# Moving the forms of w_down into the mixer stage, and splitting the loads of the last stage in place

## The chip, the cores and the metric

One core of one Trainium2 chip. The metric is the time of one launch in microseconds on the device; below, "the time" is the median of the runs, and one further execution, taken with the hardware profiler, is where every row comes from.

## The reference, cut to what matters

One decoder layer over T = 1056 tokens (1024 of a prompt and 8 sequences of 4 new ones), D = 1024, all in float32.

```python
proj = x @ w_in                              # 1024 x 4096, split into hq hf hi hg rq rk rv rg
o_h  = hgrn2(silu(hq), k(hf), hi, logf(hf))  # 4 heads, chunkwise recurrence
o_r  = retention(rotary(rq), rotary(rk), rv) # 4 heads, chunkwise recurrence
mix  = concat(rmsnorm(o_h) * silu(hg), rmsnorm(o_r) * silu(rg))
x    = layer_norm(alpha * x + mix @ w_out)
hidden = silu(x @ w_gate) * (x @ w_up)       # 1024 -> 2816
x    = layer_norm(alpha * x + hidden @ w_down)   # 2816 -> 1024
```

The outputs are y for all tokens and the recurrent states of both head groups.

## The kernel before, in words

**Arithmetic.** Everything is kept transposed: 128 features in the partitions, tokens along the free dimension. A float32 operand is split by `split` (lines 205 to 207) into `hi`, a rounded copy in fp32r made by ScalarE, and `lo`, the remainder, made by VectorE or GpSimd. A product is then three matmuls, hi·hi, hi·lo and lo·hi.

**Stages.** (1) The mixer: `proj_rqk`, `proj_v` and `proj_hqf` project, head by head; `mixer`, a generator, does a head's recurrence. `gate` multiplies in the gates. (2) The output projection `oproj`, and the first layer norm. (3) Gate and up: FF = 2816 is 22 blocks of 128, taken as 11 pairs p. Pair 0 goes by `gu`; pairs 1 to 10 by `unit`, which multiplies 2 x 2 blocks by Strassen-Winograd's method with seven products (A11·B11, S2·T2, S3·T3, S1·T1, A12·B21, A22·T4, S4·B22) for each of two token halves `pr`. A unit has 7 x 2 x 12 = 168 matmuls, a pair two units (gate, then up). `blocks` makes the seven forms of the weights of a unit: it loads two raw blocks and makes sums on GpSimd (lines 876, 877, 878, 883) and seven splits. `kinds` makes the seven forms of the hidden activations and stores them in the DRAM tile `hd`. (4) Down: for each of seven products (`DOWN`), `wkind` loads four blocks of forms of w_down from the DRAM tile `wb`, `hkind` loads 11 blocks of `hd`, both are split again, and 4 x 33 matmuls run for each half, 1848 in all. The second layer norm, `norm2`, ends it.

**Forms of w_down, before.** `prep`, with `rowsum` and `forms`, works on them during gate and up. w_down is centred (each row minus its mean, which takes the layer norm's mean away beforehand). `rowsum` loads a row block whole for its sum; `forms` loads it again in halves, centres it and stores the seven forms, 14 stores to a pair. `forward` puts a piece of this into the queue `side` ahead of each unit.

**Order.** `side` is a queue of generators; `tick` takes steps from it between the matmul groups of the main work, so the code of both is interleaved as it is written. A scheduler with a timeline model of its own then fixes the order of the instructions on each engine; at run time every engine, and the one DMA queue (SP, which issues all loads and stores), keeps that order and waits at an instruction whose inputs or buffers are not ready. `high_priority` moves instructions up.

**Buffers.** Raw weights pass through `wr`, three buffers of 512 KB used in rotation by weights, `rowsum`, `forms` and `wkind` alike. Split weights pass through the ring `bh`/`bl` of eight half blocks. In PSUM, `pj` (three banks in the mixer, four later) holds projections, `mx` the rest. `h`, 16 buffers, holds hidden blocks and, in the last stage, the loads of `hkind`.

```python
side.append(("w", forward()))            # ahead of each unit of gate and up
w = blocks(a["w_gate"], 2 * p)
```

Of the kernel before, what the change touches and what calls it, by code (L numbers as in the profile page):

```python
# [9 lines left out]
F32 = mybir.dt.float32  # L10
# [17 lines left out]
H = 4  # L28
# [110 lines left out]
def body(tc, ctx, a):  # L139
# [73 lines left out]
    def load_raw(src, shape=(P, KT, P), part=None):  # L213
        raw = wp.tile(list(shape), F32, tag="wr", name="wr", bufs=3)
        nc.sync.dma_start(raw[:, :part] if part else raw, src)
        return raw
# [38 lines left out]
    with ExitStack() as ctxA:  # L255
# [22 lines left out]
        pa.tile([P, 744], F32, name="gap")  # L278
# [38 lines left out]
        def proj(mt, chunks=[(c * CW, CW) for c in range(NC3)]):  # L317
            w = pre.pop(mt) if mt in pre else load_w(a["w_in"][mt])
            for c0, n in chunks:
                out = pj()[:, :n]  # L320
                group(out, wk(w), xk(c0, n), rate[0])
                yield slice(c0, c0 + n), out
# [54 lines left out]
        def proj_rqk(h):  # L377
            q, k = (q0, k0) if h == 0 else (slot("q", 2), slot("k", 2))
            gens = [(proj(4 * H + h), q, 1.0), (proj(5 * H + h), k, P ** -0.5)]
# [32 lines left out]
        def wmean(k):  # L412
            wrow = load_raw(a["w_or"][k].rearrange("p (k n) -> p k n", n=P)).rearrange("p k n -> p (k n)")
            mn = tmp.tile([P, 1], F32, tag="mn", name="mn", bufs=2)
            V.tensor_reduce(mn, wrow, axis=AX, op=add)
            V.tensor_scalar(mn, mn, -1.0 / D, None, op0=mul)
            S.activation(wrow, wrow, AF.Identity, bias=mn)
            nc.sync.dma_start(wc[k], wrow)
# [248 lines left out]
        mix(1, 0)  # L667
        proj_rqk(1)
        mix(1, 1)
        proj_rqk(2)  # L670
        proj_v(1, 1)
# [5 lines left out]
        for k in range(3, 6):  # L677
            wmean(k)
        proj_hqf(0)
        for k in range(6, 8):  # L680
            wmean(k)
        proj_v(0, 0)
        mix(0, 0)
        proj_hqf(1)
        mix(0, 1)
        gate(1, 0)
        proj_hqf(2)
        proj_v(0, 1)
        mix(0, 2)
        gate(1, 1)  # L690
        proj_hqf(3)
        mix(0, 3)
# [15 lines left out]
    with ExitStack() as ctxB:  # L708
# [282 lines left out]
        def rowsum(p, i):  # L991
            raw = load_raw(a["w_down"][2 * p + i].rearrange("p (k n) -> p k n", n=P))
            mn = tmp.tile([P, 1], F32, tag=f"mn{i}", name=f"mn{i}", bufs=2)
            V.tensor_reduce(mn, raw.rearrange("p k n -> p (k n)"), axis=AX, op=add)
            V.tensor_scalar(mn, mn, -1.0 / D, None, op0=mul)  # L995
            if i == 0:
                mns[p] = [mn]
            else:
                both_ = tmp.tile([P, 1], F32, tag="mnb", name="mnb", bufs=2)
                V.tensor_tensor(both_, mn, mns[p][0], op=add)  # L1000
                mns[p] += [mn, both_]

        mns = {}

        def forms(p, c):
            m1, m2, m12 = mns[p]
            raw = wp.tile([P, 2, 2, 2, P], F32, tag="wr", name="wr", bufs=3)
            for i in range(2):
                nc.sync.dma_start(raw[:, i], a["w_down"][2 * p + i].rearrange("p (j c m n) -> p j c m n", j=2, c=2, n=P)[:, :, c])
            a11, a21, a12, a22 = [raw[:, i, j] for i in range(2) for j in range(2)]  # L1010

            def put(n, src):
                nc.sync.dma_start(wb[KW.index(n), 2 * c:2 * c + 2, :, p, :].rearrange("m p n -> p m n"), src)

            def two():
                return ut()[:, :2 * P].rearrange("p (m n) -> p m n", n=P)

            yield
            s1, s2, s4 = two(), two(), two()
            V.scalar_tensor_tensor(s1, a21, m12, a22, op0=add, op1=add)  # L1020
            put("S1", s1)
            V.tensor_tensor(a21, a11, a21, op=sub)
            put("S3", a21)
            yield
            for x, mn, n in ((a22, m2, "A22"), (a12, m2, "A12"), (a11, m1, "A11")):
                S.activation(x, x, AF.Identity, bias=mn)  # L1026
                put(n, x)
            V.tensor_tensor(s2, a22, a21, op=sub)
            put("S2", s2)
            yield  # L1030
            V.tensor_tensor(s4, a12, s2, op=sub)
            put("S4", s4)

        def prep():
            for i in range(2):
                rowsum(0, i)
            for p in range(NPAIR):
                for c in range(2):
                    for _ in forms(p, c):
                        yield  # L1040
                    if p + 1 < NPAIR:
                        rowsum(p + 1, c)
                    yield
                    if 2 * p + c > 1:
                        yield True

        def wkind(n, mm):
            out = []  # L1050
            for r0, r1 in ((0, 8), (8, NPAIR)):
                raw = load_raw(wb[n, mm, :, r0:r1, :], (P, 8, P), r1 - r0)
                if cnt["w"] < 2:
                    for r in range(r0, r1, HK):
                        e = min(r + HK, r1)
                        hi, lo = [t.rearrange("p (k n) -> p k n", n=P)[:, :e - r] for t in ring()]
                        split(hi, lo, raw[:, r - r0:e - r0])
                        out += [(hi[:, k], lo[:, k]) for k in range(e - r)]
                else:
                    s = (cnt["w"] - 2) % 6  # L1060
                    hi, lo = [X[:, hl].rearrange("p k t -> p (k t)")[:, (s * NPAIR + r0) * P:(s * NPAIR + r1) * P].rearrange("p (k n) -> p k n", n=P) for hl in range(2)]
                    split(hi, lo, raw[:, :r1 - r0])
                    out += [(hi[:, k], lo[:, k]) for k in range(r1 - r0)]
# [53 lines left out]
        work = prep()  # L1117

        def forward():
            for x in work:  # L1120
                yield
                if x:
                    return

        for p in range(1, NPAIR):
# [4 lines left out]
            side.append(("w", forward()))  # L1130
# [3 lines left out]
            side.append(("w", forward()))  # L1134
# [8 lines left out]
        for x in work:  # L1143
            pass
# [104 lines left out]
```

## Time and profile before

| | us |
|---|---|
| median of 3 runs | 1417.36 (1416.13 to 1419.42) |
| the profiled execution, its own time | 1416.91 |
| its span, first to last instruction | 1414.8 |
| PE busy in the span | 1307.9 (92%) |
| DVE, ACT, POOL busy | 793.9, 527.7, 688.5 |

PE is TensorE, PEld its weight loads, DVE VectorE, ACT ScalarE, POOL GpSimd, SPq the DMA queue on SyncE. A row of the timeline is: start, length, engine, line, operation, output tile <- inputs, shapes, count, and in brackets the idle time of the engine before it with what ended it. A granted clock of 1.00 is 2.4 GHz, of 0.50 1.2 GHz; a number between is a mean of these over a stretch. Instructions that overlap the edge of a window are counted in both windows.

### The profile page before, as it was taken

To read this page: it belongs to the slowest core of one execution; us is meant where nothing else is said; L and a number is where in the kernel's file an instruction comes from. 1 tells how busy PE (TensorE), PEld (TensorE's weight loads), DVE (VectorE), ACT (ScalarE), POOL (GpSimd) and SP (SyncE) were. 2 spreads that over 40 slices of the span, in tenths; PEclk is the share of its full clock that TensorE was granted. 3 is DMA by queue.
4 is the path that set the end of the run, shared out by engine and by line. 5 is a ranking of instruction groups with operands and counts; after the bars stand their busy time and mean duration, and the time that the engine had idled before them with its cause. 6 is when DMAs were issued, how large, how long until landed. Compare 5 with 4: busy or idle time off the path is not lost. (4 is left out here: it accounts for less than half of the span.)

```text
span 1414.8 us, 29994 instructions
## 1 busy us (share of the span) xinstructions
PE 1307.9 (92%) x11622; PEld 1276.2 (90%) x11622; DVE 793.9 (56%) x1759; ACT 527.7 (37%) x1192; POOL 688.5 (49%) x666
## 2 busy tenths in 40 slices
PE   8999999999999999999489889989999947999997
PEld 7999999899999999999479889989989937999997
DVE  6254643756666653876637545755665557543534
ACT  6242433323232342755132322233233343444553
POOL 2762421220222263737366775866676615666550
PEclk9999999999999999999799999999999978999998
DMA  7354311111221262222745445455546486566621
GB/s 266 131 187 166 122 48 58 66 48 49 77 62 34 61 174 84 76 81 75 236 142 185 154 151 176 159 171 173 166 152 194 137 248 188 177 197 186 183 92 62
DMA packets 173789, 190.71 MB, mean 135 GB/s; under 512 B 14800, under 2 KB 154960, under 8 KB 173648
## 3 DMA queue, kind: packets, MB, share of 16 engines
q1 hardware_dynamic: 173648, 188.81, 42.5%
q8 instruction: 91, 1.49, 0.5%
q14 instruction: 50, 0.41, 0.1%
HBM read 130.20 MB, written 58.56 MB: 133 GB/s over the span
## 5 line engine op out<-in xcount | busy, mean ns | idle before, releaser
L207 POOL TENSOR_TENSOR bl<-wr,bh 128x512 fp32r<-128x512 f32 x212 | 279.9, 1333 | 366.2 <-ACT bh L206 347.8
L242 PE MATMUL pj<-X,bh 128*128 128x352 f32 (+1 forms) x1936 | 427.4, 310 | 4.8 <-DVE q L388 3.3
L242 PEld LDWEIGHTS pj<-X,bh 128*128 128x128 f32 x1936 | 321.0, 189 | 9.4 <-issue 3.6
L242 PE MATMUL pj<-X,bl 128*128 128x352 f32 (+1 forms) x968 | 297.8, 308 | 0.1
L206 ACT CAST bh<-wr 128x512 fp32r<-128x512 f32 x226 | 134.6, 617 | 236.9 <-PE pj L242 67.6
L1156 PE MATMUL pj<-XB,X 128*128 128x264 f32 x1716 | 210.6, 285 | 0.0
L1156 PEld LDWEIGHTS pj<-XB,X 128*128 128x128 f32 x1716 | 209.2, 189 | 0.0
L242 PEld LDWEIGHTS pj<-X,bl 128*128 128x128 f32 x968 | 183.0, 189 | 0.8 <-DVE bl L207 0.4
L207 POOL TENSOR_TENSOR XB<-h,XB 128x264 fp32r<-128x264 f32 x154 | 123.3, 842 | 108.2 <-ACT XB L206 108.2
L901 PE MATMUL pj<-X,bh 128*128 128x264 f32 x672 | 126.3, 288 | 21.2 <-ACT bh L206 21.2
L901 PEld LDWEIGHTS pj<-X,bh 128*128 128x128 f32 x672 | 105.0, 190 | 21.8 <-ACT bh L206 21.6
L901 PE MATMUL mx<-XB,bh 128*128 128x264 f32 x608 | 114.6, 288 | 2.5 <-DVE mn L995 1.9
L901 PE MATMUL mx<-X,bh 128*128 128x264 f32 x608 | 114.3, 288 | 0.2 <-DVE mn L995 0.2
L901 PE MATMUL pj<-XB,bh 128*128 128x264 f32 x352 | 76.2, 317 | 26.3 <-ACT bh L206 26.3
L901 PEld LDWEIGHTS mx<-XB,bh 128*128 128x128 f32 x608 | 95.5, 192 | 3.4 <-DVE mn L995 2.5
L1026 ACT ACTIVATE wr<-wr,mn 128x256 f32<-128x256 f32 x66 | 32.5, 508 | 174.8 <-DMA wr<-in_w_down 83.0
L242 PE MATMUL pj<-bh,X 128*128 128x256 f32 x512 | 96.5, 284 | 0.0
L901 PE MATMUL pj<-X,bl 128*128 128x264 f32 x336 | 95.3, 286 | 0.1
L901 PEld LDWEIGHTS mx<-X,bh 128*128 128x128 f32 x608 | 94.5, 190 | 0.6 <-DVE mn L995 0.5
L207 DVE TENSOR_TENSOR X<-wr,X 128x1024 fp32r<-128x1024 f32 (+1 forms) x52 | 65.6, 1270 | 46.2 <-ACT X L206 35.8
L901 PEld LDWEIGHTS pj<-XB,bh 128*128 128x128 f32 x352 | 63.0, 218 | 28.5 <-ACT bh L206 28.5
L901 PE MATMUL mx<-X,bl 128*128 128x264 f32 x304 | 85.9, 285 | 1.8 <-POOL bl L207 1.8
(227 smaller groups left out, 2385.3 us busy)
## 6 DMA issues: line engine op xcount, KB each, us to landing
hd<-h SPq DMA_DIRECT2D x154, 132.0 KB, 1.9
h<-hd SPq DMA_DIRECT2D x154, 132.0 KB, 2.9
wr<-wb SPq DMA_DIRECT2D x28, 512.0 KB, 4.2
wr<-in_w_in SPq DMA_DIRECT2D x23, 512.0 KB, 3.7
wr<-in_w_gate SPq DMA_DIRECT2D x22, 512.0 KB, 4.1
wr<-in_w_up SPq DMA_DIRECT2D x22, 512.0 KB, 3.8
wr<-in_w_down SPq DMA_DIRECT2D x22, 512.0 KB, 3.6
wr<-in_w_down SPq DMA_DIRECT2D x44, 256.0 KB, 4.3
```

The lines of the kernel that those rows point to most:

```text
L206: S.copy(hi, src)
L207: (eng or V).tensor_tensor(lo, src, hi.bitcast(F32), op=sub)
L242: PE.matmul(out, l, r, start=(i == 0), stop=(i == n - 1))
L901: PE.matmul(bank[pr], l[:, k], rs[k][r], start=(first and n == 0), stop=(n == 3 * HK - 1), skip_group_check=not first)
L1026: S.activation(x, x, AF.Identity, bias=mn)
L1156: PE.matmul(out, l, r, start=(i == 0), stop=(i == 3 * NPAIR - 1))
```

## The change

1. `wforms(p)`, new, makes the forms of w_down of pair p between the heads of the mixer stage, eleven calls written into the list that orders the heads. It loads the two row blocks once (512 KB each, into `wr`), centres each with `center_rows` (the body of `wmean`, which stays in use for w_out), stores three forms as they are, makes the four others on GpSimd (one into the new tile `f1`, three in place) and stores them: 7 stores of 256 KB.
2. `rowsum`, `forms`, `prep`, `forward` and their places in gate and up are taken out.
3. `again` replaces `split` for the loads of the last stage: the DMA writes into the `lo` tile itself, ScalarE makes `hi` from it, and the remainder is made in place. So `wkind` needs no `wr` buffer and makes one load of 704 KB where it made two (the first two calls three loads into the ring), and `hkind` needs no `h` buffer. A load now waits until the matmuls that read the old content of that tile are done.
4. In `hkind` the remainders of the first 11 blocks, and of every second one of the next 11, are made on DVE instead of GpSimd.
5. In the first head's rotary projections the last three of six products go to `mx` banks instead of `pj`.

```diff
+        f1 = pa.tile([P, HK, P], F32, name="f1")
+        pa.tile([P, 232], F32, name="gap")
...
+        def proj(mt, chunks=[(c * CW, CW) for c in range(NC3)], banks=(None,) * NC3):
             w = pre.pop(mt) if mt in pre else load_w(a["w_in"][mt])
+            for (c0, n), bank in zip(chunks, banks + (None,)):
+                out = (bank or pj)()[:, :n]
...
+            b1, b2 = ((pj, pj, mx), (pj, mx, mx)) if h == 0 else ((pj,) * NC3,) * 2
+            gens = [(proj(4 * H + h, banks=b1), q, 1.0), (proj(5 * H + h, banks=b2), k, P ** -0.5)]
...
+        def center_rows(w):
+            flat = w.rearrange("p k n -> p (k n)")
             mn = tmp.tile([P, 1], F32, tag="mn", name="mn", bufs=2)
+            V.tensor_reduce(mn, flat, axis=AX, op=add)
             V.tensor_scalar(mn, mn, -1.0 / D, None, op0=mul)
+            S.activation(flat, flat, AF.Identity, bias=mn)
+
+        def wforms(p):
+            w1, w2 = [load_raw(a["w_down"][2 * p + i].rearrange("p (k n) -> p k n", n=P)) for i in range(2)]
+            a11, a21, a12, a22 = w1[:, :HK], w1[:, HK:], w2[:, :HK], w2[:, HK:]
+            def put(n, src):
+                nc.sync.dma_start(wb[KW.index(n), :, :, p, :].rearrange("m p n -> p m n"), src)
+            for w in (w1, w2):
+                center_rows(w)
+            put("A11", a11)
+            put("A12", a12)
+            put("A22", a22)
+            G.tensor_tensor(f1, a21, a22, op=add)
+            put("S1", f1)
+            G.tensor_tensor(a21, a11, a21, op=sub)
+            put("S3", a21)
+            G.tensor_tensor(a11, f1, a11, op=sub)
+            put("S2", a11)
+            G.tensor_tensor(a12, a12, a11, op=sub)
+            put("S4", a12)
...
         mix(1, 0)
+        wforms(0)
         proj_rqk(1)
         mix(1, 1)
+        wforms(1)
         proj_rqk(2)
+        wforms(2)
...
         proj_hqf(3)
+        wforms(10)
         mix(0, 3)
...
-        def rowsum(p, i):
...
-        def forms(p, c):
...
-        def prep():
...
+        def again(hi, lo, src, eng):
+            raw = lo.bitcast(F32)
+            nc.sync.dma_start(raw, src)
+            S.copy(hi, raw)
+            eng.tensor_tensor(lo, raw, hi.bitcast(F32), op=sub)

         def wkind(n, mm):
...
-                raw = load_raw(wb[n, mm, :, r0:r1, :], (P, 8, P), r1 - r0)
...
+                    s = (cnt["w"] - 2) % 6
+                    hi, lo = [X[:, hl].rearrange("p k t -> p (k t)")[:, s * NPAIR * P:(s + 1) * NPAIR * P] for hl in range(2)]
+                again(hi, lo, wb[n, mm, :, r:e, :].rearrange("p r n -> p (r n)"), V)
...
         def hkind(n, pr):
-                raw = hid(F32)
-                nc.sync.dma_start(raw, hd[n, pr, r])
...
-                split(hi, lo, raw, G)
+                again(hi, lo, hd[n, pr, r], V if cnt["h"] < NPAIR or cnt["h"] < 2 * NPAIR and r % 2 else G)
...
-            side.append(("w", forward()))
             w = blocks(a["w_gate"], 2 * p)
...
-            side.append(("w", forward()))
             unit(blocks(a["w_up"], 2 * p), (0, 1), up_fin(h, p), RF)
...
-        for x in work:
-            pass
```

## Rows read from the trace of the kernel before

**Rows 1.** The stages, by windows of the span. Columns: window, its length; then busy time and instructions of PE, PEld, DVE, ACT and POOL; granted TensorE clock; mean busy share of the DMA engines; GB/s.

```profile
25.00:475.00 450.00, 447.36 (x4867) 426.82 (x4866) 246.06 (x681) 152.54 (x329) 134.59 (x138) 1.00 0.27 87
690.00:715.00 25.00, 4.20 (x19) 3.90 (x20) 13.91 (x21) 2.71 (x7) 15.59 (x18) 0.52 0.62 199
...
715.00:1136.00 421.00, 385.07 (x2985) 379.43 (x2984) 245.92 (x419) 129.47 (x291) 291.00 (x234) 0.96 0.52 163
1136.00:1190.00 54.00, 24.16 (x172) 23.53 (x171) 35.09 (x42) 23.74 (x50) 25.04 (x35) 0.74 0.78 233
```

**Rows 2.** The chain that ended last, one stretch in the last stage, where PE runs matmuls of 264 columns with nothing else in between: start, length, what, count.

```profile
1358.48 36.77 PE pj L1156 x303
```

**Rows 3.** PE's timeline, from the end of pair 1 to the end of the hand-over to the last stage: the matmuls with an idle time before them that tell the periods apart, and the last one of pair 1 and of pair 10.

```profile
687.45 0.28 PE L901 MATMUL mx<-X,bl 128*128 128x264 f32 x1
...
710.69 1.25 PE L901 MATMUL pj<-X,bh 128*128 128x264 f32 x4 [21.20 <-ACT bh L206]
...
786.01 0.81 PE L901 MATMUL pj<-XB,bh 128*128 128x264 f32 x2 [3.54 <-ACT bh L206]
...
837.89 1.25 PE L901 MATMUL pj<-XB,bh 128*128 128x264 f32 x4 [4.88 <-ACT bh L206]
...
1075.27 0.51 PE L901 MATMUL pj<-XB,bh 128*128 128x264 f32 x2 [1.65 <-ACT bh L206]
...
1120.67 0.50 PE L901 MATMUL pj<-XB,bh 128*128 128x264 f32 x2 [1.76 <-ACT bh L206]
...
1139.52 0.28 PE L901 MATMUL mx<-X,bl 128*128 128x264 f32 x1
1160.83 0.81 PE L1156 MATMUL pj<-XB,bh 128*128 128x264 f32 x2 [21.04 <-ACT XB L206]
...
1187.82 0.78 PE L1156 MATMUL pj<-XB,bh 128*128 128x264 f32 x2 [8.80 <-DVE Y L1165]
```

**Rows 4.** Waits of PE, by line and releaser: total us, times, longest. The first row is of 690 to 1136 us (gate and up), the second, after the dots, the largest of 25 to 475 us (the mixer; its three rows add up to 2.4 us).

```profile
PE pj L901 <- ACT bh L206: 47.5, 11, 21.2
...
PE mx L652 <- DVE tk L625: 0.9, 1, 0.9
```

**Rows 5.** Waits of the DMA queue SP itself in 610 to 1140 us: total us, times, longest.

```profile
SPq L1013 <- DMA wr<-in_w_down: 51.9, 18, 4.8
SPq L215 <- POOL bl L207: 42.2, 18, 8.8
SPq L1013 <- ACT wr L1026: 34.5, 22, 4.8
```

**Rows 6.** SP's timeline in the long idle time of PE after pair 1.

```profile
699.91 3.88 SPq L961 DMA_DIRECT2D hd<-h  x5
...
704.86 0.92 SPq L215 DMA_DIRECT2D wr<-in_w_gate  x2
```

**Rows 7.** One set of weight forms from its load to its first and its last use: two rows of the chain (pair 10, up), and POOL's last split of the set in its timeline.

```profile
1110.52 5.33 DMA wr<-in_w_down
...
1120.69 1.28 POOL bl L207
...
1129.31 1.29 POOL L207 TENSOR_TENSOR bl<-wr,bh 128x512 fp32r<-128x512 f32 x1 [0.73 <-ACT bh L206]
```

**Rows 8.** Groups of instructions of one shape: line, engine, operation, tiles, shapes, count | busy us, mean ns of one | idle time before them and what ended it.

```profile
L207 POOL TENSOR_TENSOR bl<-wr,bh 128x512 fp32r<-128x512 f32 x212 | 279.9, 1333 | 366.2 <-ACT bh L206 347.8
L207 POOL TENSOR_TENSOR XB<-h,XB 128x264 fp32r<-128x264 f32 x154 | 123.3, 842 | 108.2 <-ACT XB L206 108.2
...
L206 ACT CAST XB<-h 128x264 fp32r<-128x264 f32 x154 | 55.4, 411 | 33.4 <-PE pj L1156 19.9 <-issue 10.7 <-DMA h<-hd 2.4
...
L790 POOL TENSOR_TENSOR Y<-Y,s 128x264 f32<-128x264 f32 x32 | 27.2, 883 | 2.3 <-ACT s L1142 2.3
...
L994 DVE TENSOR_REDUCE mn<-wr 128x1 f32<-128x1024 f32 x22 | 26.8, 1218 | 48.2 <-DMA wr<-in_w_down 48.2
...
L417 ACT ACTIVATE wr<-wr,mn 128x1024 f32<-128x1024 f32 x8 | 9.2, 1152 | 13.3 <-DVE mn L416 10.8 <-issue 1.2 <-POOL sg L387 1.1
```

**Rows 9.** The largest wait of SP in the mixer, 25 to 475 us: the store of a head's state waits for the recurrence.

```profile
SPq L590 <- DVE S L588: 133.4, 8, 32.1
```

**Rows 10.** The first rotary head: PE's wait for a PSUM bank within the first 30 us, and, after the dots, the window behind it.

```profile
PE pj L242 <- DVE q L388: 3.3, 1, 3.3
...
25.00:28.20 3.20, 3.20 (x13) 3.20 (x12) 2.81 (x10) 1.50 (x4) 0.24 (x1) 0.50 1.04 380
```

**Rows 11.** The hand-over to the last stage: the landing of the last store of hidden blocks, in the chain; SP's issue of the loads behind it; POOL and DVE in their timelines.

```profile
1153.96 5.70 DMA hd<-h
...
1154.95 12.29 SPq L1071 DMA_DIRECT2D h<-hd  x22
...
1160.85 25.04 POOL L207 TENSOR_TENSOR XB<-h,XB 128x264 fp32r<-128x264 f32 x35 [30.25 <-ACT XB L206]
...
1171.80 14.51 DVE L207 TENSOR_TENSOR X<-wr,X 128x384 fp32r<-128x384 f32 x1 [10.59 <-ACT X L206]
```

**Rows 12.** DMA issues: what, queue, operation, count, KB each, median us from issue to landing.

```profile
hd<-h SPq DMA_DIRECT2D x154, 132.0 KB, 1.9
h<-hd SPq DMA_DIRECT2D x154, 132.0 KB, 2.9
...
wc<-wr SPq DMA_DIRECT2D x8, 512.0 KB, 3.3
```

More of the change, by code (lines that the diff above doesn't have):

```diff
@@ L211, in ring, with load_raw @@
         return [wp.tile([P, HK * P], F32R, tag=t, name=t, bufs=RING) for t in ("bh", "bl")]
-    def load_raw(src, shape=(P, KT, P), part=None):
+    def load_raw(src, shape=(P, KT, P)):
         raw = wp.tile(list(shape), F32, tag="wr", name="wr", bufs=3)
-        nc.sync.dma_start(raw[:, :part] if part else raw, src)
+        nc.sync.dma_start(raw, src)
         return raw
@@ L276, in body @@
         csts.append(pa.tile([P, a["csm"].shape[1]], F32, name="csm"))
-        pa.tile([P, 744], F32, name="gap")
+        f1 = pa.tile([P, HK, P], F32, name="f1")
+        pa.tile([P, 232], F32, name="gap")
         xr = [slot(f"M{k}", 1) for k in range(KT)]
@@ L412, in wmean @@
         def wmean(k):
-            wrow = load_raw(a["w_or"][k].rearrange("p (k n) -> p k n", n=P)).rearrange("p k n -> p (k n)")
+            w = load_raw(a["w_or"][k].rearrange("p (k n) -> p k n", n=P))
+            center_rows(w)
+            nc.sync.dma_start(wc[k], w.rearrange("p k n -> p (k n)"))
+        def center_rows(w):
+            flat = w.rearrange("p k n -> p (k n)")
             mn = tmp.tile([P, 1], F32, tag="mn", name="mn", bufs=2)
-            V.tensor_reduce(mn, wrow, axis=AX, op=add)
+            V.tensor_reduce(mn, flat, axis=AX, op=add)
             V.tensor_scalar(mn, mn, -1.0 / D, None, op0=mul)
-            S.activation(wrow, wrow, AF.Identity, bias=mn)
-            nc.sync.dma_start(wc[k], wrow)
+            S.activation(flat, flat, AF.Identity, bias=mn)
[5 more added lines that the diff above has]
+            for w in (w1, w2):
+                center_rows(w)
+            put("A11", a11)
[9 more added lines that the diff above has]
+            put("S4", a12)
         def msplit(gi, sl):
@@ L678, in body @@
             wmean(k)
+        wforms(3)
         proj_hqf(0)
@@ L681, in body @@
             wmean(k)
+        wforms(4)
         proj_v(0, 0)
         mix(0, 0)
+        wforms(5)
         proj_hqf(1)
         mix(0, 1)
+        wforms(6)
         gate(1, 0)
+        wforms(7)
         proj_hqf(2)
+        wforms(8)
         proj_v(0, 1)
         mix(0, 2)
+        wforms(9)
         gate(1, 1)
         proj_hqf(3)
+        wforms(10)
         mix(0, 3)
@@ L987, in gu @@
                 V.tensor_tensor(f, po[1], sg, op=mul)
-        def rowsum(p, i):
[L992 to L1001, printed above, removed]
@@ L1003, in body @@
-        mns = {}
-        def forms(p, c):
[L1006 to L1032, printed above, removed]
@@ L1034, in prep @@
-        def prep():
[L1035 to L1045, printed above, removed]
+        def again(hi, lo, src, eng):
+            raw = lo.bitcast(F32)
+            nc.sync.dma_start(raw, src)
+            S.copy(hi, raw)
+            eng.tensor_tensor(lo, raw, hi.bitcast(F32), op=sub)
@@ L1049, in wkind @@
         def wkind(n, mm):
             out = []
-            for r0, r1 in ((0, 8), (8, NPAIR)):
-                raw = load_raw(wb[n, mm, :, r0:r1, :], (P, 8, P), r1 - r0)
+            for r in range(0, NPAIR, HK if cnt["w"] < 2 else NPAIR):
                 if cnt["w"] < 2:
[L1054 to L1058, printed above, removed]
+                    e = min(r + HK, NPAIR)
+                    hi, lo = [t[:, :(e - r) * P] for t in ring()]
@@ L1059, in wkind @@
                 else:
+                    e = NPAIR
                     s = (cnt["w"] - 2) % 6
-                    hi, lo = [X[:, hl].rearrange("p k t -> p (k t)")[:, (s * NPAIR + r0) * P:(s * NPAIR + r1) * P].rearrange("p (k n) -> p k n", n=P) for hl in range(2)]
-                    split(hi, lo, raw[:, :r1 - r0])
-                    out += [(hi[:, k], lo[:, k]) for k in range(r1 - r0)]
+                    hi, lo = [X[:, hl].rearrange("p k t -> p (k t)")[:, s * NPAIR * P:(s + 1) * NPAIR * P] for hl in range(2)]
@@ L1064, in wkind @@
+                again(hi, lo, wb[n, mm, :, r:e, :].rearrange("p r n -> p (r n)"), V)
+                out += [(hi[:, k * P:(k + 1) * P], lo[:, k * P:(k + 1) * P]) for k in range(e - r)]
             cnt["w"] += 1
@@ L1116, in body @@
                 side.insert(min(len(side), 1 if q == 1 else NQ), (("c1", q // 2), combine1(q // 2)))
-        work = prep()
-        def forward():
-            for x in work:
-                yield
-                if x:
-                    return
         for p in range(1, NPAIR):
@@ L1142, in body @@
                 S.copy(mc, mu)
-        for x in work:
-            pass
         last = []
```

4 lines of the change are left out of this document (removed).

## The prediction

> **What bounds the kernel now.** I read the windows by stage first, then PE's waits, then PE's timeline at the two places where it stands still longest, and last what the queues did there. PE sets the time. One 264-column matmul, back to back, takes 36.77 / 303 = 0.1213 us [rows 2], and that pace is the measure for what follows. In the mixer PE is busy 447 of 450 us, its waits add up to 2.4 us, and DVE, ACT and POOL are busy 55%, 34% and 30% [rows 1, 4]: room there, on every engine but PE. In gate and up it is different. From the last matmul of pair 1 (687.7) to the last of pair 10 (1139.8) are 452.1 us [rows 3]; nine pairs of 336 matmuls are 3024 x 0.1213 = 366.8, the small mean products about 2. **83 us are lost**, of which 21.2 in one hole, at 689.5 to 710.7. PE's waits in this stretch name one cause, ACT's cast of a weight form: 47.5 us in 11 waits, the hole among them [rows 4]. The granted clock is 0.52 in the window of the hole and 0.96 in the rest of the stage [rows 1]: the clock fell to 1.2 GHz behind the longer waits, and that is the remainder of the loss.
>
> Why are the casts late? In the hole SP issues stores of hidden blocks and of forms one behind the other, and the load of the next gate block goes out only at 704.9 [rows 6]. Over the whole stage SP itself waits 51.9 and 34.5 us at line 1013, the stores of the w_down forms, and 42.2 us at line 215, a raw load that waits for a `wr` buffer [rows 5]. Forms and unit weights share one in-order queue and three buffers. POOL is busy 291 of 421 us in this stage [rows 1], close behind PE.
>
> At the hand-over to the last stage PE stands 21.0 us, runs a little, and stands 8.8 us more [rows 3]. From 1139.8 to the end of the last matmul at 1401.1 are 261.3 us; 1848 x 0.1213 = 224.2, side products about 3.4, so **34 us are lost** here. The chain shows the order: last store of hidden blocks issued at about 1153.5, landed at 1159.7, the loads behind it; meanwhile the 22 loads are issued one by one over 12.3 us, POOL then makes 35 remainders in a row over 25.0 us, and a DVE remainder of the weights takes 14.5 us beside it [rows 11].
>
> **The change, part by part.**
>
> *First head, `mx` banks.* PE waits 3.3 us for a `pj` bank that the rotary products hold, and the 3.2 us window behind it runs at a granted clock of 0.50, which is another 1.6 us [rows 10]. With three `mx` banks the fourth product need not wait; it reads tokens that the third already read. The fifth needs the last third of x, whose split ends about when the fourth product has just begun. I take -4.9 us; bounds 0 (x or the first `pj` of `proj_v` is late instead) and -4.9.
>
> *Forms in the mixer.* Eleven calls add 22 loads, 22 reductions of 1.22 us on DVE, 22 centrings of 1.15 us on ACT, 44 sums on POOL (128x512, as the split remainder of that size, 1.33 us) and 77 stores [rows 8]: DVE 27 us, ACT 25 us, POOL 59 us. DVE goes from 246 to 273 of 450 us, POOL from 135 to 194; DMA traffic rises by 11 x (1.0 + 1.8) MB, some 70 GB/s beside 87 [rows 1]. The cover is PE's work in the mixer and the ring, which holds four weights ahead. The nearest precedent is `wmean`: eight loads, reductions, centrings and stores run in this stage already, and PE's waits there are 2.4 us in all [rows 4]. What is new is that POOL waits: the third sum overwrites a block whose store must have been read out, 3.3 us by the store of w_out's rows [rows 12], and behind POOL's sum stand the remainders of the next weights and, in heads 1 to 3, a rotary product that holds a `pj` bank. Three such heads, some 2 us each not hidden, make +6. Bounds: 0, as with `wmean`; and 11 x (2 x 1.22 of DVE + one longest wait behind a store) at half exposure, 11 x 5.7 / 2 = +31.
>
> *Gate and up without forms.* Taken from SP in this stage are 66 loads and 154 stores, from DVE and ACT their work on them, from `wr` all but the unit weights. The hole goes: what stood ahead of the gate load was a piece of `prep` three times the usual size. What then sets the pace? From 1110.5, with the loads of a set out, POOL's remainder of S2 is done at 1122.0 and that of the last form at 1130.6: 20.1 us [rows 7], with the buffer then free for the second load of the next unit, about 0.4 us for its issue. A unit of 168 matmuls is 20.4 us. So this chain stands level with PE, and it gets shorter by the part of the load that was slowed by the forms' traffic (5.3 us against about 4). Between 1075.3 and 1120.7, a pair without `center`, the period is 45.4 us where PE needs 40.8; between 786.0 and 837.9, one with it, 51.9 [rows 3]. `center` is 8 x 0.88 = 7.1 us of POOL [rows 8]. After the change I expect a plain pair at 1 us over PE's time and one with `center` at 4 over, since about 3 of its 7 us fit where POOL waits for loads: five plain pairs and four with it, 5 + 16, and 3 us at the start. So 24 of the 83 us stay: **-59 us**. Bounds: -83, PE never waits; and -28, only the hole with its clock goes: seven pairs from 786.0 to 1120.7 take 334.7 us where 286 are needed, 7 lost in each, 55 in the eight from pair 3 on, and 83 less these are 28.
>
> *Hand-over.* The loads no longer follow 35 splits on POOL: of the first 22 remainders DVE makes 16 and POOL 6. The tiles of T2 and T3 that the first 11 loads fill come free after the second and third product of the last unit, so ten of the eleven can be in place before it ends. What stays is the last block: its store lands in 1.9, its load in 2.9 us [rows 12], cast and remainder 0.4 and up to 0.8 [rows 8], against 30 matmuls or 3.6 us on the ten before it. With the issues between them that is about 4 us of wait if SP is free; with SP behind the last pair's stores and the lower clock after it I take 11 us lost of 34: **-22 us**. Bounds: -30 (4 stay) and -3, if the loads still stand behind the last store on SP. The queue must take 4 + 11 loads in any case, and all but the ring's now wait for PE where they used to wait for a buffer.
>
> The DVE remainder of 14.5 us [rows 11] bears on this. The Trainium skill (SBUF — State Buffer, section "Who interferes with whom") says that DVE and GpSimd share a port pair by an exclusive lock: a DVE instruction with two SBUF inputs and a GpSimd one that reads SBUF do not overlap, the later one stands still. The trace agrees: that remainder ended when POOL's row of 35 did. By the rule the 16 and the 6 follow one another, at POOL's 0.72 us each 22 x 0.72 = 16 us, against 16 x 0.72 = 12 if they overlapped; and the page speaks against the mixer part too, where 59 us of POOL sums would hold up DVE's recurrence.
>
> *The rest of the last stage.* In-place loads wait for PE to be done with a tile. 24 tiles hold two products' blocks, so a set has one product time, 4 x 33 x 0.1213 = 16 us, for load (2.9) and 11 remainders on POOL (11 x 0.84 = 9.3) [rows 8, 12]: 12.2 us fit. I put 0; if they did not fit, each of 12 later sets would show a wait.
>
> **The sum.** -4.9 + 6 - 59 - 22 = -80 us. The profiled execution took 1416.9 us by its own time (span 1414.8), half a microsecond below the median, so the sum goes from 1417: **1337 us**.
>
> **The rivals.**
>
> *The chain of the unit weights keeps the pace.* Speaks for it: POOL has the largest load after PE in this stage, and 20.1 us against 20.4 leaves nothing [rows 1, 7]. Against: SP's waits at line 1013, 86 us, go in any case [rows 5]. Only the hole goes then, -28 instead of -59: **1368 us**. Chance 0.20.
>
> *The hand-over stays.* For it: the order on SP is fixed beforehand, and the stores of `kinds` have high priority. -3 instead of -22: **1356 us**. Chance 0.12.
>
> *Everything lost in gate and up is the forms'.* -79 there and -28 at the hand-over, the mixer as with `wmean`: 1417 - 4.9 - 79 - 28 = **1305 us**. Chance 0.13.
>
> *Slower: the forms block the mixer.* One mechanism, SP in order. SP waits there 133 us for heads' states, up to 32.1 us at once [rows 9]. If such a store stands between a call's loads and its stores, POOL waits at the third sum as long, and with it the remainders of the next weights, beyond what the ring holds. At an average wait of 16.7 us (133.4 / 8) [rows 9] in each of 11 calls it costs 184 us, less the 86 gained elsewhere: **1515 us**. It decides from 86 / 11 = 7.8 us a call. Against: the ring's four weights cover more than that, and `wmean` stood in the same queue at no cost. Chance 0.05.
>
> My forecast has 0.50. **Range** 1303 to 1373: it takes in the forecast's own bounds in part, the fast case and both slower savings, and leaves out the blocked mixer and the ends of the mixer's cost. A measurement of this kernel can tell about 0.2%, 3 us, from no change. Faster has the first three cases and the forecast, 0.94; slower 0.05; same 0.01.
>
> **What would show it.** In the profile after: no PE wait over 5 us between pair 1 and pair 10, plain pairs within 42 us; PE's waits in the mixer under 10 us in all; no 14 us remainder and less than 12 us of PE's idle time at the hand-over; no wait at the fourth product. It would be wrong if POOL's sums stood waiting for stores while PE waited for a weight in the mixer, or if the pairs kept 45 us with POOL never idle.

## The result, and the profile after

The kernel after takes **1324.9 us** in the median of 4 runs (1321.4 to 1328.1) against 1418.1 us before; the ratio is 0.934, its 95% interval 0.932 to 0.937. The forecast was 1337 us with a range of 1303 to 1373. The profiled execution of after has a span of 1322.7 us, 92.1 less than before. The stages of the two profiles, cut where PE (TensorE) starts the first product of pair 1 and where it ends the last products of pair 10 and of the last stage:

| stage | before, us | after, us | difference | forecast |
|---|---|---|---|---|
| first head | | | -4.9 (measured alone, first experiment) | -4.9 |
| up to pair 1, from 641.8 with the banks alone | 646.6 | 666.6 | +24.8 | +6 |
| pairs 1 to 10 | 493.2 | 410.6 | -82.5 | -59 |
| from there to the last product | 261.3 | 231.8 | -29.5 | -22 |

The windows of the same stages in the kernel after, in the columns of [rows 1]:

```profile
25.00:475.00 450.00, 426.87 (x4680) 405.35 (x4679) 273.99 (x693) 166.46 (x335) 189.05 (x181) 0.98 0.50 156
667.00:1077.00 410.00, 410.00 (x3366) 409.73 (x3365) 209.44 (x374) 134.01 (x283) 323.65 (x268) 1.00 0.32 104
1077.00:1102.00 25.00, 20.73 (x169) 20.30 (x168) 24.74 (x45) 13.82 (x26) 13.45 (x14) 1.00 0.89 295
1102.00:1309.00 207.00, 207.00 (x1716) 207.00 (x1715) 89.64 (x184) 90.61 (x192) 107.45 (x132) 1.00 0.50 159
```

In gate and up PE is busy in all of 410 us, at a granted clock of 1.00, where it was 0.96 and 0.52 in the hole [rows 1]. The mixer pays: PE is idle for 23 of its 450 us, where it was for 2.6 [rows 1]. PE's largest waits there, 25 to 520 us (total, times, longest):

```profile
PE mx L610 <- ACT tk L593: 7.3, 4, 3.8
PE mx L497 <- DVE ain L526: 5.5, 3, 2.7
PE mx L497 <- DVE k L522: 2.6, 2, 2.2
PE pj L242 <- ACT v L354: 2.2, 2, 1.7
PE mx L681 <- DVE tk L654: 1.9, 1, 1.9
```

All of PE's waits there add up to 22.7 us, against 2.4 before. None of these is a weight that comes late. All but one row are small products of the recurrence that wait for DVE or for ACT (whose `tk` copies a transposed `k`); the row of line 242 is a projection that waits for ACT's copy out of its `pj` bank. The waits are some 20 of the 24.8 us. The rest goes with the clock: it is 0.50 in four short stretches of this stage, 13.7 us together, each within 1.5 us of the end of such a wait; from 291.0 to 294.2, two products of 352 columns take 0.79 us instead of 0.48. At the hand-over [rows 3], PE's timeline of after shows no idle time between the last product of pair 10 and the first of the last stage, and two short waits behind:

```profile
1076.91 0.28 PE L941 MATMUL mx<-X,bl 128*128 128x264 f32 x1
1077.03 0.40 PE L1127 MATMUL pj<-XB,bh 128*128 128x264 f32 x2
...
1087.33 0.39 PE L1127 MATMUL pj<-XB,bl 128*128 128x264 f32 x1 [2.62 <-DVE bl L1035]
...
1097.76 0.52 PE L1127 MATMUL pj<-XB,bh 128*128 128x264 f32 x2 [1.65 <-DVE Y L1136]
```

### The profile page after: what moved, and what is told of

It reads as the page before. It is cut to its first block, busy times and chain, and to the rows that moved or that the text cites. A ratio compares the mean times of both kernels' runs of the same rounds, so it can differ in the third digit from the quotient of the medians.

```text
span 1322.7 us, 29630 instructions
## 1 busy us (share of the span) xinstructions
PE 1281.9 (97%) x11622; PEld 1255.1 (95%) x11622; DVE 735.1 (56%) x1650; ACT 525.0 (40%) x1122; POOL 733.2 (55%) x694
## 4 chain that ended last, share of the span: by engine, by line
PE 80%; DMA 9%; DVE 5%; ACT 2%; issue 2%; POOL 2%; SPq 1%; ACTq 0%; POOLq 0%; DVEq 0%
PE pj L242 25%; PE mx L941 17%; PE pj L1127 16%; PE pj L941 14%; DMA wr<-in_w_in 2%; DMA wc<-wr 2%; DMA wb<-wr 1%; PE mx L640 1%; DMA wr<-in_w_down 1%; PE mx L610 1%; PE mx L497 1%; PE mx L242 1%; PE mx L642 1%; DVE mn L423 1%; DMA wr<-in_w_v 1%
## 5 line engine op out<-in xcount | busy, mean ns | idle before, releaser
L242 PE MATMUL pj<-X,bh 128*128 128x352 f32 (+1 forms) x1888 | 417.3, 309 | 4.6 <-ACT v L354 2.2
L242 PEld LDWEIGHTS pj<-X,bh 128*128 128x128 f32 x1888 | 313.9, 189 | 9.4 <-ACT v L354 2.6
L242 PE MATMUL pj<-X,bl 128*128 128x352 f32 (+1 forms) x944 | 290.9, 308 | 0.1
L206 ACT CAST bh<-wr 128x512 fp32r<-128x512 f32 x220 | 131.6, 619 | 284.1 <-POOL wr L918 70.9
L242 PEld LDWEIGHTS pj<-X,bl 128*128 128x128 f32 x944 | 178.4, 189 | 1.0 <-DVE bl L207 0.4
L1035 POOL TENSOR_TENSOR XB<-XB 128x264 fp32r<-128x264 f32 x138 | 114.8, 867 | 105.0 <-ACT XB L1034 104.4
L941 PEld LDWEIGHTS pj<-X,bh 128*128 128x128 f32 x672 | 104.3, 188 | 0.3
L941 PE MATMUL mx<-XB,bl 128*128 128x264 f32 x304 | 86.2, 283 | 0.0
L242 PEld LDWEIGHTS pj<-bh,X 128*128 128x128 f32 x512 | 80.0, 190 | 1.8 <-issue 1.5
L1034 ACT CAST XB<-XB 128x264 fp32r<-128x264 f32 x154 | 57.3, 411 | 39.8 <-PE pj L1127 20.5
L423 DVE TENSOR_REDUCE mn<-wr 128x1 f32<-128x1024 f32 x30 | 36.5, 1216 | 64.1 <-DMA wr<-in_w_down 47.2
```

What stands on the lines that cost most here:

```text
L206: S.copy(hi, src)
L242: PE.matmul(out, l, r, start=(i == 0), stop=(i == n - 1))
L423: V.tensor_reduce(mn, flat, axis=AX, op=add)
L941: PE.matmul(bank[pr], l[:, k], rs[k][r], start=(first and n == 0), stop=(n == 3 * HK - 1), skip_group_check=not first)
L1034: S.copy(hi, raw)
L1035: eng.tensor_tensor(lo, raw, hi.bitcast(F32), op=sub)
```

## The experiments

All runs in one table: where pair 1 starts, how long pairs 1 to 10 take, how long it is from there to the end of the last product (all from the trace), the median time, and the ratio to the kernel before with its interval. The first three columns are of one execution each; where the mixer is the same code (before, e3, e9, e11), pair 1 starts at 645.9 to 647.9, so differences of some 2 us there say nothing.

| run | pair 1 starts | pairs 1-10 | rest | median | ratio |
|---|---|---|---|---|---|
| before | 646.6 | 493.2 | 261.3 | 1418.1 | |
| after | 666.6 | 410.6 | 231.8 | 1324.9 | 0.934 [0.932, 0.937] |
| e1_banks | 641.8 | 494.6 | 258.9 | 1410.2 | 0.996 [0.994, 0.999] |
| e2_forms | 673.5 | 410.6 | 245.9 | 1343.5 | 0.949 [0.944, 0.955] |
| e3_inplace | 645.9 | 493.3 | 230.8 | 1387.1 | 0.981 [0.976, 0.986] |
| e4_pool | 667.1 | 410.6 | 229.0 | 1322.3 | 0.934 [0.930, 0.939] |
| e5_nosum | 657.2 | 410.6 | 233.0 | 1321.8 | 0.931 [0.929, 0.934] |
| e6_nocenter | 670.1 | 410.6 | 231.6 | 1326.2 | 0.935 [0.933, 0.937] |
| e9_free_store | 647.9 | 474.8 | 253.8 | 1389.2 | 0.979 [0.976, 0.982] |
| e11_nosumload | 647.7 | 449.6 | 249.8 | 1363.5 | 0.963 [0.960, 0.966] |
| e8_late | 675.2 | 410.6 | 233.2 | 1336.0 | 0.943 [0.941, 0.945] |
| e8_vlate | 673.8 | 410.6 | 232.8 | 1331.3 | 0.939 [0.936, 0.941] |
| e12_oneload | 662.6 | 410.6 | 232.7 | 1319.0 | 0.931 [0.927, 0.936] |
| e13_transfers | 642.0 | 410.6 | 233.1 | 1302.6 | 0.920 [0.917, 0.923] |

**The parts one by one.** Part 5 alone:

```
 before
-                out = pj()[:, :n]
+                out = (bank or pj)()[:, :n]
...
+            b1, b2 = ((pj, pj, mx), (pj, mx, mx)) if h == 0 else ((pj,) * NC3,) * 2
```

> The kernel before with part 5 alone (three of the first head's six rotary products in mixer banks). Theory: the wait of 3.3 us at the fourth product and the one of about 1.6 us behind it go, the first product of proj_v starts at 31.6 us instead of 36.6 and everything behind it keeps its distance: -5 us, about 1412. Rival: the mixer banks so taken make the first transposes wait, and the gain is given back before 60 us: 1416 to 1419.

Pair 1 starts 4.9 us earlier. The median falls by 7.6 against the runs of before beside it; the interval, 2 to 9 us, holds the 5. The theory stands.

The forms alone, the last stage and the banks as before (of the edit, the hidden blocks' loads are shown):

```
 after
-                again(hi, lo, hd[n, pr, r], V if cnt["h"] < NPAIR or cnt["h"] < 2 * NPAIR and r % 2 else G)
+                raw = hid(F32)
+                nc.sync.dma_start(raw, hd[n, pr, r])
+                split(hi, lo, raw, G)
...
```

> The kernel before with the forms of w_down made between the mixer heads, but its own loads of the last stage (through wr and h, the splits of the activations on GpSimd) and its own banks. Theory: the mixer costs +25 us, pairs 1 to 10 give -82.5, and of the 29.5 us of the hand-over only the third that hung on SP's queue and on the forms' last stores comes (-9), since the 35 GpSimd operations ahead of the second group stay: about 1351. Rival: the whole of the hand-over was SP's queue behind the forms' stores: about 1330.

Parts 3 and 4 alone, the in-place loads with the splits on DVE (forms still in gate and up):

```
 before
+        def again(hi, lo, src, eng):
...
-                raw = hid(F32)
-                nc.sync.dma_start(raw, hd[n, pr, r])
-                split(hi, lo, raw, G)
+                again(hi, lo, hd[n, pr, r], V if cnt["h"] < NPAIR or cnt["h"] < 2 * NPAIR and r % 2 else G)
```

> The kernel before with parts 3 and 4 alone: loads of the last stage split in place, the first activations' splits on DVE; the forms are made in the gate/up stage as before. Theory: gate/up and mixer unchanged, the first product of the last stage not earlier (the forms' last stores still stand in SP's queue), the GpSimd wait of 21 us in the second group shortens to under 3: about -18, 1399. Rival: the loads still come behind the forms' stores, so DVE's splits start as late as GpSimd's did: 1412 to 1417.

And the kernel after with part 4 undone:

```
 after
-                again(hi, lo, hd[n, pr, r], V if cnt["h"] < NPAIR or cnt["h"] < 2 * NPAIR and r % 2 else G)
+                again(hi, lo, hd[n, pr, r], G)
```

> The kernel after with all splits of the activations left on GpSimd (part 4 undone, loads still in place). Theory: 11 splits at about 0.84 us are 9.3 us for a stage whose first group multiplies for 16 us, and SP's queue is free now, so GpSimd falls behind in the first group only: +5 to +10, 1330 to 1335. Rival 1: GpSimd was the whole of the hand-over, +20, 1345. Rival 2: with the queue free GpSimd keeps up: 1325.

The forms alone give the whole 82.5 us of pairs 1 to 10 and, with the banks as before, cost 26.8 in the mixer. At the hand-over both theories missed, since two different changes reach the same loss: the forms' move gives 15.3 us of it, the in-place loads give 30.5 by themselves, with the forms' stores still in the queue. Splitting on GpSimd alone (e4) is no worse than splitting on DVE: rival 2 there. The first loads of hidden blocks on SP, and PE's first product, in e2_forms and then in e3_inplace, where the last unit ends at 1084.1 and at 1139.2:

```profile
1094.79 0.50 SPq L1051 DMA_DIRECT2D h<-hd  x1
...
1098.57 0.81 PE L1124 MATMUL pj<-XB,bh 128*128 128x264 f32 x2 [14.47 <-ACT XB L206]
```

```profile
1120.79 0.33 SPq L1051 DMA_DIRECT2D XB<-hd  x1
...
1121.71 3.38 SPq L1013 DMA_DIRECT2D wb<-wr  x3
...
1138.92 0.29 PE L901 MATMUL mx<-X,bl 128*128 128x264 f32 x1
1139.05 0.40 PE L1157 MATMUL pj<-XB,bh 128*128 128x264 f32 x2
```

Into a buffer `h`, the first load goes out 10.7 us after the last unit ended; into its tile of XB, 18.4 us before it ends. XB's tiles are free after the second and third product of the unit, while the hidden blocks use the `h` buffers to the end. That the buffers set the place of the load is argued, not shown: in e2_forms the first load shows no wait of its own, it stands in SP's order right behind stores of hidden blocks. The run also changes place and split together; e4 says that the engine of the split doesn't matter, but says it in the kernel after.

**Why gate and up was slow.** Two runs of the kernel before, one for SP's waits at the forms' stores, one for the three `wr` buffers:

```
 before, e9_free_store
-                nc.sync.dma_start(wb[KW.index(n), 2 * c:2 * c + 2, :, p, :].rearrange("m p n -> p m n"), src)
+                nc.sync.dma_start(wb[KW.index(n), 2 * c:2 * c + 2, :, p, :].rearrange("m p n -> p m n"), Y[:, 0, :2 * P].rearrange("p (m n) -> p m n", n=P))
 before, e11_nosumload
-            raw = load_raw(a["w_down"][2 * p + i].rearrange("p (k n) -> p k n", n=P))
...
-            V.tensor_reduce(mn, raw.rearrange("p k n -> p (k n)"), axis=AX, op=add)
+            V.tensor_reduce(mn, K_("mean"), axis=AX, op=add)
```

> The kernel before with the 154 form stores of the gate/up stage taken from a tile that is always there, so that SP no longer waits at them for DVE's, ACT's and the loads' results; number and size of the stores stay, the forms stored are not those of w_down. Theory S, SP's waits at these stores (52 + 34 us) make the loads of the unit weights late: pairs 1 to 10 fall from 493 us to 430 or less, about 1355. Rival B, the three wr buffers shared with 66 more loads (and the DMA traffic) are the cause: above 475, about 1400 to 1417.

> The kernel before with the 22 loads of whole w_down rows left out that serve the row sums alone (the sums are taken of a constant tile, so the centring is wrong; forms, their 44 loads and 154 stores stay). Rival B, the wr buffers: a third of the forms' claims on them goes, pairs 1 to 10 fall by 25 us or more, about 1390. Theory S, the waits at the stores: the loads left out are not those that the stores wait for, under 10 us, 1407 to 1417.

Of 82.5 us, the stores' waits give 18.4 (the stores read another tile there, so a `wr` buffer no longer waits to be read out either) and the 22 loads for the row sums alone 43.6. Rival B fits both runs, with 474.8 us in the one where it said above 475; theory S has the smaller part. The other 20.5 us, and whether the two parts overlap, no run shows. SP's largest wait at line 215 in the kernel without waits at the stores, 600 to 1140 us, beside 42.2 us before [rows 5]:

```profile
SPq L215 <- POOL bl L207: 105.5, 22, 11.5
```

SP's time moved from the stores to the loads that want a buffer. Without the row sums' loads PE's waits for ACT's cast fall from 47.5 us in 11 waits [rows 4] to this (600 to 1200 us); the longest, 14.8, is the hole, now 3 us into pair 2:

```profile
PE pj L901 <- ACT bh L206: 17.4, 2, 14.8
```

SP's waits at the stores stay in that run, 47.3 and 35.5 us for loads and for ACT, and the DMA engines move as much as before, 165 GB/s against 164 (690 to 1130 us). So of what a row-sum load takes, neither of these was the lever; the buffer is what is left, together with the load's place on SP and DVE's shorter reductions, and no run parts these. Neither run closes the hole: without the stores' waits its 21.2 us become two waits of 3.5 and 9.9 us.

**Why the mixer pays.** Two theories from the trace of after. M1: the centring is in order on DVE and ACT, and waits for its load. At 277.94 two reductions of DVE have stood 3.2 us for their loads; behind them stands the product `q`, whose input from ACT (line 367) has been there since 278.2, and PE waits 2.19 us for what `q` and `k` become (DVE, ACT, PE):

```profile
277.94 2.48 DVE L423 TENSOR_REDUCE mn<-wr 128x1 f32<-128x1024 f32 x2 [3.20 <-DMA wr<-in_w_down]
280.33 0.51 DVE L368 TENSOR_TENSOR q<-pj,sg 128x352 f32<-128x352 f32 x1
...
277.75 0.46 ACT L367 ACTIVATE sg<-pj 128x352 f32<-128x352 f32 x1
...
281.72 0.45 PE L497 MATMUL mx<-q,k 128*32 128x16 f32 x32 [2.19 <-DVE k L522]
```

M2: GpSimd's sums hold DVE. DVE's product `k*f`, usually 0.41 us, takes 1.48 beside line 446, the product of `f` before it 1.20 instead of 0.27 beside line 444, and PE waits for what follows them (DVE, POOL, PE):

```profile
286.84 1.20 DVE L523 TENSOR_TENSOR f<-f 128x64 f32<-128x64 f32 x1
287.96 0.41 DVE L521 TENSOR_TENSOR q<-q,f 128x256 f32<-128x256 f32 x1
288.30 1.48 DVE L522 TENSOR_TENSOR k<-k,f 128x256 f32<-128x256 f32 x1
...
286.39 1.53 POOL L444 TENSOR_TENSOR wr<-f,wr 128x512 f32<-128x512 f32 x1 [0.47 <-DMA wb<-wr]
287.99 1.50 POOL L446 TENSOR_TENSOR wr<-wr 128x512 f32<-128x512 f32 x1
...
289.92 0.45 PE L497 MATMUL mx<-q,k 128*32 128x16 f32 x32 [2.55 <-DVE ain L526]
```

```
 after, e5_nosum
-            G.tensor_tensor(f1, a21, a22, op=add)
...
-            G.tensor_tensor(a12, a12, a11, op=sub)
 after, e6_nocenter
-            for w in (w1, w2):
-                center_rows(w)
```

> The kernel after with the four GpSimd sums of each set of forms left out (the raw blocks are stored in place of S1 to S4, so the last stage multiplies other numbers; loads, centring and all 77 stores stay). Theory M2, GpSimd's sums hold DVE still through the port they share, and take GpSimd from the weights' remainders: PE's waits behind DVE's q, k and GpSimd's tiles in the mixer go with their clock, the mixer's 25 us of extra time fall to about 10, 1310. Rival M1, the centring's place in DVE's and ACT's order: the waits stay, 1320 to 1325.

> The kernel after with the row reductions and centrings of the forms left out (22 reductions of 1.22 us on DVE, 22 casts of 1.15 us on ACT; sums and stores stay, the forms are of uncentred weights). Theory M1, what stands behind a reduction or centring that waits for its load is late (v's copies, bh's casts, q and k): half or more of the mixer's extra 25 us go, about 1310. Rival M2, the sums' lock: 1320 to 1325. If both this and the run without sums gain about 12, the two share it.

Neither stands as expected. Without the sums pair 1 starts 9.4 us earlier, but the median time can't be told from that of after (the profiled execution was the fastest of its four, 4.7 us below their median); without the centring it starts 3.6 us later. PE's waits (25 to 520 us) are 13.4 us without the sums and 23.1 without the centring, so either kind of work alone makes PE wait. With the sums alone the longest wait is for GpSimd itself:

```profile
PE mx L407 <- POOL sg L401: 5.0, 1, 5.0
```

The next three runs asked for other causes: a crowded place, the claim on `wr`.

```
 after, e8_late (e8_vlate: every call three places later again)
         mix(1, 0)
-        wforms(0)
...
         proj_hqf(0)
+        wforms(0)
...
 after, e12_oneload
-            w1, w2 = [load_raw(a["w_down"][2 * p + i].rearrange("p (k n) -> p k n", n=P)) for i in range(2)]
+            w1 = w2 = load_raw(a["w_down"][2 * p].rearrange("p (k n) -> p k n", n=P))
...
-            for w in (w1, w2):
-                center_rows(w)
+            center_rows(w1)
```

> The kernel after with the eleven sets of forms moved to later heads: the first stands behind the projections of hgrn head 0, not behind the first retention head, and the others follow at every projection, mixer and gate up to head 3's. Nothing else differs. Theory D, the sets are crowded: in the kernel after all eleven are loaded by 368 us, where the DMA engines are busy 75, 67 and 57% of the first three hundred us, and the unit weights' loads stand behind them; moved into the calmer part, the mixer's extra 25 us fall under 10, 1305 to 1312. Rival E, it is each set's own work that costs, wherever it stands: 1320 to 1328.

> As the run before, with the sets moved later again: from the projections of hgrn head 1 to the gate of hgrn head 0. Theory D: as good as the run before or better, 1300 to 1310, unless the sets now meet the loads of w_out and of the first gate and up weights behind the mixer, which would show as waits between 520 and 650 us. Rival E: 1320 to 1328.

> The kernel after with one load of w_down in each set instead of two (both rows' forms are made of the first row's weights, so the last stage multiplies other numbers): 11 loads, 11 reductions and 11 centrings fewer, the 44 sums and 77 stores stay. Theory W, what the mixer pays for is the claim on the three wr buffers, two of which each set holds through loads, centring and stores: about half of the 25 us go, 1310 to 1314. Rival T, it is traffic: the loads left out are 11 of some 60 half-megabyte transfers that the sets make, so a fifth goes, about 1320.

Theory D falls: in the calm part the sets cost 33.5 and 32.0 us instead of 24.8. I take the reason to be the hgrn heads that they meet there: DVE is busy 76 us of 100 in both runs (300 to 400 us). What the sets do to DVE is plainest in e8_late. A 9-column operation of DVE, otherwise 0.17 us, stands 4.29 us until GpSimd's row of four instructions ends (first lines DVE, then POOL, then PE):

```profile
385.61 4.29 DVE L233 TENSOR_TENSOR nt<-sq,ny 128x9 f32<-128x9 f32 x1
389.82 0.33 DVE L665 SCALAR_TENSOR_TENSOR ss<-ss,f,mx 128x128 f32<-128x128 f32 x1
390.08 0.16 DVE L234 SCALAR_TENSOR_TENSOR nt<-nt,ny 128x9 f32<-128x9 f32 x1
...
384.85 1.30 POOL L444 TENSOR_TENSOR wr<-f,wr 128x512 f32<-128x512 f32 x1
386.10 2.55 POOL L207 TENSOR_TENSOR bl<-wr,bh 128x512 fp32r<-128x512 f32 x2
388.60 1.28 POOL L446 TENSOR_TENSOR wr<-wr 128x512 f32<-128x512 f32 x1
...
392.45 1.97 PE L681 MATMUL mx<-cst,tk 128*128 128x128 f32 x8 [3.64 <-DVE tk L654]
```

One load instead of two takes 4.0 us off the mixer, a sixth of 24.8, and the time, 1319.0 us, is near T's; but half of the reductions and centrings went with the loads. The last run leaves out both of what e5 and e6 left out singly:

```
 after
-            for w in (w1, w2):
-                center_rows(w)
...
-            G.tensor_tensor(f1, a21, a22, op=add)
-            put("S1", f1)
-            G.tensor_tensor(a21, a11, a21, op=sub)
+            put("S1", a21)
...
-            G.tensor_tensor(a11, f1, a11, op=sub)
...
-            G.tensor_tensor(a12, a12, a11, op=sub)
```

> The kernel after with both the sums and the centring of the forms left out: of each set only the two loads and the seven stores of 256 KB remain (raw blocks are stored, so the last stage multiplies other numbers). Rival X, the price in the mixer is that of the transfers, of the claim on the three wr buffers and of SP's order: the first product of pair 1 stays 15 us or more behind the 641.8 us that the run with the banks alone showed, 1315 to 1322. Theory Y, it is the work on DVE, ACT and GpSimd, and each half of it was enough to make the other's waits: under 8 us behind, about 1305.

Theory Y stands. Pair 1 starts at 642.0, 0.2 us behind the kernel with the banks alone: 22 loads and 77 stores cost the mixer nothing, nor do the `wr` buffers for as long as these hold them. In the kernel after the work holds the buffers longer, which no run shows by itself; but there too PE waits for no weight. Its window and its two largest waits of PE (25 to 520 us):

```profile
25.00:475.00 450.00, 444.84 (x4871) 423.21 (x4870) 251.87 (x688) 153.16 (x330) 137.91 (x140) 1.00 0.50 159
```

```profile
PE mx L604 <- ACT tk L587: 1.7, 2, 1.0
PE pj L242 <- DVE q L391: 1.2, 2, 0.7
```

The DMA engines are as busy as in the kernel after (0.50, 159 and 156 GB/s), and PE is idle for 5 us, not 23. The price is the work on DVE, ACT and GpSimd. A single stretched operation isn't the price: `k*f` takes up to 1.52 us in this run too, and PE doesn't wait behind it. The parts don't add: with the centring there, the sums cost 9.4 us (666.6 - 657.2), without it 28.1 (670.1 - 642.0); without the sums, the centring costs 15.2 (657.2 - 642.0). By the medians the sums cost 3.1 us with the centring there and 23.6 without it, the centring 19.2 without the sums and nothing with them. In each run the scheduler also orders the rest anew, which is part of these differences.

## Why the prediction was right in its time, and where its steps were wrong

**The sum** is right by two errors that oppose each other. -4.9 + 24.8 - 82.5 - 29.5 = -92.1 where -80 stood. The mixer's price was 19 us too small, the gains 23.5 and 7.5 too small; that they cancel in part is luck.

**First head: right**, in place and size. In e1 PE's wait of 3.3 us at the fourth product is gone.

**Forms in the mixer: the mechanism was wrong, and so the size.** The step said that POOL's third sum waits for a store's readout, some 2 us in three heads. In the trace of after all of POOL's waits for such stores add up to 2.2 us (1.67 at 268.61 and 0.47 at 286.39), and e13 shows that all loads and stores together are free. The term should have been the work itself on DVE, ACT and GpSimd. The step read "room there, on every engine but PE" off the busy shares [rows 1], but a share says nothing of a short operation that must be done at once because PE waits for it. The rule of the shared port stood in the prediction, as a rule that speaks against this part, and no term was made of it. The 2 us a head had no row behind them. The upper bound, +31, held. Of the signs that the prediction named, one came out against it: PE's waits in the mixer, which were to stay under 10 us, are 22.7. The others held.

The Trainium skill (SBUF — State Buffer, section "Who interferes with whom") says that a DVE operation with two SBUF inputs contends with a GpSimd one that reads SBUF, and that the one that comes later stands still. The rows at 288.30 (kernel after) and 385.61 (e8_late) agree. The same section says that a reduction on trn2 never contends. The 30 reductions of the mixer agree: 14 of them ran beside a GpSimd instruction, and minimum, median and maximum of one are, in ns (kernel after):

```profile
L423 DVE TENSOR_REDUCE mn<-wr x30: 1200/1220/1222, 31.4 to 368.0; 128x1 f32<-128x1024 f32 x30
```

**Gate and up: right in what goes, wrong in what stays.** The step expected that the chain of the unit weights, 20.1 us and the issue of the next load against PE's 20.4 [rows 7], would keep a plain pair at 1 us over PE's time and one with `center` at 4. Nothing stayed. The prediction also put all of the loss beyond the 47.5 us down to the clock. In that stretch of the kernel before, PE's other waits are 10.7 us (6.8 of them for POOL's remainders); PE was busy 393.8 us for 368.8 us of work, so the clock's part is 25. As to the chain, the step closed that loop at the last remainder of a set. Four loads on SP (the second block of an up set, the two of the next gate set, the first of the up set after) and the last two remainders of that first set on POOL, in the kernel after:

```profile
991.61 0.33 SPq L215 DMA_DIRECT2D wr<-in_w_up  x1
994.66 0.33 SPq L215 DMA_DIRECT2D wr<-in_w_gate  x1
1012.04 0.33 SPq L215 DMA_DIRECT2D wr<-in_w_gate  x1
1014.98 0.33 SPq L215 DMA_DIRECT2D wr<-in_w_up  x1
...
1010.72 1.29 POOL L207 TENSOR_TENSOR bl<-wr,bh 128x512 fp32r<-128x512 f32 x1 [0.26 <-ACT bh L206]
1013.66 1.29 POOL L207 TENSOR_TENSOR bl<-wr,bh 128x512 fp32r<-128x512 f32 x1 [1.65 <-ACT bh L206]
```

The gate set's second load goes out at 1012.04, when the last but one remainder has freed its buffer (1010.72 + 1.29), not at the end of the last, and its first block was on its way to the third buffer from 994.66. So load and work overlap, and the period is PE's, 1012.04 - 991.61 = 20.4 us. POOL has 324 us of work in 410 and waits for ACT in between, so `center` fits as well. The third buffer, which the forms' loads took, is by e11 what the chain lacked most, as far as the runs part it from the place on SP: a third of these loads gone gives 43.6 us.

**Hand-over: the size was near its bound (-30), the reason wrong in part.** It was put on the 16 splits that DVE takes over and on SP's queue. By e4 the DVE splits are worth nothing, and by e3 the in-place loads, with these splits, give all of it with the forms' stores still in the queue. The part of the step on the tiles of T2 and T3, free after the second and third product, was the one that counted. "SP behind the last pair's stores" is what failed: 15 loads of hidden blocks go out before the last unit ends at 1077.2, ahead of the stores that begin at 1072.96 (kernel after):

```profile
1060.16 2.28 SPq L1033 DMA_DIRECT2D XB<-hd  x5
...
1063.93 2.33 SPq L1033 DMA_DIRECT2D XB<-hd  x5
...
1072.96 0.32 SPq L1001 DMA_DIRECT2D hd<-h  x1
...
1089.69 4.60 SPq L1001 DMA_DIRECT2D hd<-h  x8
```

The 4 us that stay, 2.62 and 1.65, are the size of the step's bound but not its wait: they end with a weight's remainder and with a sum on DVE, not with the last hidden block. (34 less 11 is also 23, not the 22 of the step.)

**The rest of the last stage: right**, PE is busy in 207.00 of 207 us.

**The rivals.** "Everything lost in gate and up is the forms'" was nearest: its 1305 us lacks just the mixer's price, and is the time of e13 within 3 us. The slower case didn't come; in the mixer of after POOL waits 2.2 us for stores in all, and PE for no weight.

**Open.** How the 24.8 us divide between the sums and the centring isn't settled, since each hides the other. A placing of the sets that hides this work wasn't found: two later ones were worse, and no run that computes everything beat the kernel after by more than the measurement can tell.

## What to carry to other kernels

Before work is moved into a stage "with room", look there for short operations that another engine waits for, and price the new work by what it does to these, not by the busy shares. In a chain that loads, works and frees, find the buffer that the next load really waits for; it can come free before the last step, and one more user of the buffers can cost more than waits in the queue (43.6 against 18.4 us here). Where two changes can remove the same wait, try each alone: here half of the hand-over's gain came with one and all of it with the other, and the two don't add. When a sum comes out right, check its terms one by one: here two errors of some 19 and 31 us hid each other in part.

## What the runs showed of the hardware that was not expected

In e8_late DVE didn't get its turn between two GpSimd instructions: at 385.61 it stood 4.29 us, past the ends of three GpSimd instructions (line 444 and two of line 207) that followed one another without a pause, and was done when the fourth was, at 389.9. So the price of one such meeting is the length of GpSimd's row, as it was for the remainder of 14.5 us beside a row of 35 [rows 11]. Heavy transfers did no harm: at 159 GB/s, with the DMA engines half busy, the mixer of e13 starts pair 1 at 642.0 us, against 641.8 in e1 with 88 GB/s.
